# MLP weight preparation in three streams instead of one, with a bound on low parts per unit

## The chip, the cores and the metric

The kernel runs on one core of a Trainium2 chip. The metric is the device time of one execution in microseconds. The core has five engines with a queue of their own each: TensorE (PE in the profile, with its weight loads as PEld), VectorE (DVE), ScalarE (ACT), GpSimd (POOL) and SyncE (SP), which here only issues transfers. Each engine executes its queue in the order in which the program was written; engines wait for one another by semaphores.

## The reference

One layer of an encoder on 1024 tokens of width 1024. All arithmetic is float32.

```python
u = rms_norm(x, norm1_g); proj = u @ w_in            # 1024 x 5120
...                                                  # attention, short convolution, gates
x = x + merged @ w_o
h = rms_norm(x, norm2_g) @ w_mlp_in                  # 1024 x 4096
x = x + jnp.square(jax.nn.relu(h)) @ w_mlp_out       # 4096 x 1024
```

The change touches only the last two lines, the MLP.

## The kernel before, in words

**Arithmetic.** Each float32 operand is split into a high and a low float16 part, and a product is taken as three products of parts (high-high, high-low, low-high). Both MLP products also go through a scheme with seven products of half-size blocks instead of eight; sums of blocks are formed before it, on weights and activations, and sums of results after it. So weights have to be prepared before TensorE can use them, and that preparation runs beside the matmuls of the work before.

**First product.** `w_mlp_in` is cut into 16 chunks, numbered 0 to 15. A chunk is computed by `quad(q)`: seven units, each a group of 12 matmuls of 512 columns into one of eight PSUM banks (`seven`, `unit`, L207). Chunks 0 and 1 go in two halves of 256 columns each (chunk 0, chunk 1, chunk 0, chunk 1), because the activations come in pairs of tokens. The seven results are taken out of PSUM in the order of units 0 to 6: a copy by ScalarE (L1613), then by VectorE L1594 (unit 1), L1599 (unit 2), none for unit 3, L1615 (unit 4), L1602 to L1604 (unit 5, which read the banks of units 5, 3 and 2) and L1607 (unit 6). A bank is used again eight allocations later. Behind unit 6 `h_done` issues, on the next units, Relu (L1559) and Square (L1561) on ScalarE, four sums (L1281) on GpSimd, for chunks 0 and 1 on VectorE, and a store of 1.8 MB to memory by SP (L1572). The result tile of a chunk is one of two buffers.

**Preparation of a chunk.** `sums1(q)`: scale the rows of the two weight tiles (eight ScalarE operations, L959), square and add them up (two, L968), four block adds on GpSimd (L1077), then three units later the sum column on VectorE (L939, L940). `scale_of`: some units later a one-column matmul with ones (L198) adds over the partitions; it takes a PSUM bank of its own from the same rotation. A unit later VectorE turns the sum into a power of two (L201, L437 to L444). `prep1(q)` then waits by `gate(q)` until the weight buffer is free (three buffers, so until chunk q - 3 has been emitted) and `forms_split` writes the parts: four high parts on ScalarE and four low parts on VectorE, alternating (L1094, L1090). Behind the second low part SP gets the loads of the next weight tiles (`load_upto`, L229; five tile buffers).

**Second product.** `prep2(s)`, s = 0 to 3, makes 28 operand pairs, seven for each s: squares (L1666, L1669), block sums on GpSimd (L1675, L1676), a scale as above, and for each pair a high and low part of the activations (L1701, L1703) and two halves of the weights (L1706, L1710). The activations of the second pair come by a load of their own (L1682). Each pair is used by four units, which start behind chunk 15.

**What sets the order.** The program is written by Python generators: `fg` holds those that finish work on results, `bg` those that prepare weights. After emitting the 12 matmuls of a unit, `unit` emits the evacuation of the unit before and then lets `fg` advance by some steps and `bg` by some ticks (two steps and five ticks in the first product). A tick advances the first generator of `bg`. If that yields `WAIT` and the flag `side` is set, the tick goes to the next generator; otherwise it is used up. `apart(mark, n)` yields `WAIT` until n units have been emitted since mark. In the kernel before, `side` is off in the MLP, and `bg` holds one sequence: `sums1(2)`, then `prep1(2)` with `sums1(3)` at its end, and so on to 15. `first2()` and `prep2(0)` are appended behind chunk 13.

Of the kernel before, what the change touches and what calls it, by code (L numbers as in the profile page):

```python
# [10 lines left out]
F32 = mybir.dt.float32  # L11
F16 = mybir.dt.float16
# [58 lines left out]
def encoder_block(ctx: ExitStack, tc: tile.TileContext, x, weights, cols, gqk, rel, masks, out):  # L71
# [66 lines left out]
    WAIT = "w"  # L138
# [35 lines left out]
        forced[0] = False  # L174

    late, units, forced, side, splitting = [], [0], [False], [False], [False]
    work = [0]

    def apart(mark, n=3, of=units):
        while of[0] < mark + n and not forced[0]:  # L180
            yield WAIT
# [22 lines left out]
    def unit(mms, post=None, steps=0, ticks=0):  # L204

        for ps, l, r, a, b in mms:
            T.matmul(ps, l, r, start=a, stop=b)  # L207
        units[0] += 1
        work[0] += len(mms) * mms[0][0].shape[-1]
        settle()  # L210
        if post:
            late.append(post)
        for i in range(max(steps, ticks)):
            if i < steps:
                step()
            if i < ticks:
                tick()

    def settle():
# [864 lines left out]
    def parts(todo, s, then):  # L1084

        prev = None
        for n, it in enumerate(todo + [None]):
            if prev:
                o, w = prev
                V.scalar_tensor_tensor(o(1), w, sc[:, s], o(0), op0=OP.mult, op1=OP.subtract)  # L1090
                then(n - 1)
            if it:
                o, w = it
                A.activation(o(0), w, AF.Copy, scale=sc[:, s])  # L1094
            prev = it
            yield
# [245 lines left out]

    def gate(i):
        while pe_done[0] < i - 2:
            yield

    def need(i):
        while i not in ready:
# [23 lines left out]
    def prep1(q):  # L1372

        ch = c1[q]
        s, ch.inv = yield from scale_of(ch.sum, 9, 1)
        yield from gate(q)
        pool, tag = TAGS[q % 3]
        P = P1[q] = pool.tile([128, 7 if q else 8, 2, 512], F16, name="w16_1", tag=tag)
        yield from forms_split(ch, tsum[q], s, P)
        ready.add(q)  # L1380
        if 1 < q < 15:
            yield from sums1(q + 1)

    SQJ = U2[1][:, 0, :, :, 384:512].rearrange("p s k t -> p (s k) t").bitcast(BF16)
    scaled = []
# [143 lines left out]
    def last_pair():  # L1529
        sq(7, 1)()  # L1530
        normal(7, row3(7))
        yield from wait(3)
        form_sums()
        high(3, 0), high(3, 1)
        yield from wait(6)
        low(3, 0)
        yield from wait(3)
        bg.append(sums1(2))
        bg.extend(prep1(q) for q in range(2, 16))
        yield from wait(6)  # L1540
        low(3, 1)
        limit[0] = 10 ** 6
        load_upto(done[0] + 5)
# [10 lines left out]
    def h_done(q, c0=0, c1=512, wait1=0, wait2=0):  # L1554

        f = AS[q] if c1 < 512 else AS.pop(q)
        v = f[:, :, c0:c1]
        yield from wait(wait1)
        A.activation(v[:, 0:4], v[:, 0:4], AF.Relu)  # L1559
        yield  # L1560
        A.activation(v[:, 0:4], v[:, 0:4], AF.Square, scale=sc[:, c1w[q].inv],  # L1561
                     accum_out=sc[:, at(bsum[q // 4], 4 if c1 < 512 else q % 4)])
        yield
        yield from wait(wait2)
        if q > 1:
            yield from sums(v, G)
        else:
            for _ in sums(v, V):
                pass
        if c1 < 512:  # L1570
            return
        SP.dma_start(HS[q // 4][:, :, q % 4], f)  # L1572
        live.remove(q)
        if q % 4 == 3:
            m = tmp()
            V.tensor_reduce(sc[:, m], sc[:, bsum[q // 4]], axis=AX, op=OP.max)
            yield
            yield from pow2(m, 14, *R[q // 4])
            r_ready[q // 4] = True

    def quad(q, c0=0, c1=512):
        need(q)
        if c0 == 0:
            while q - 2 in live:
# [12 lines left out]

        def post5(ps):
            V.tensor_tensor(z[1], ps[5], z[5], op=OP.subtract)  # L1599

        def post7(ps):
            V.tensor_tensor(z[6], ps[7], z[5], op=OP.add)  # L1602
            V.tensor_tensor(z[2], ps[4], z[6], op=OP.add)  # L1603
            V.tensor_tensor(z[3], ps[5], z[6], op=OP.subtract)  # L1604

        def post3(ps):
            V.tensor_tensor(z[1], ps[3], z[1], op=OP.add)  # L1607
            if q == 0:
                fg.append(h_done(q, c0, c1, 3, 4 if c0 else 24))
            elif c1 == 512:  # L1610
                fg.append(h_done(q, 0, c1, *((2, 6) if q == 1 else ())))
        seven(P1[q], actU2, c0, c1, {
            1: lambda ps: A.activation(z[4], ps[1], AF.Copy),  # L1613
            6: post6, 5: None if c0 else post5,
            2: lambda ps: V.tensor_tensor(z[0], ps[2], z[4], op=OP.add),  # L1615
            7: post7, 3: post3}, 2 if c1 == 512 else 3, 5, (1, 2, 5, 4, 6, 7, 3) if c0 else (1, 6, 5, 4, 2, 7, 3))

    def whole(q):
        quad(q)
        pe_done[0] = q + 1  # L1620
# [7 lines left out]
    quad(1, 256, 512)  # L1628
    pe_done[0] = 2
    held[0] = 0  # L1630
    for q in range(2, 14):
        whole(q)


    OPS, X2 = {}, {}
# [12 lines left out]

    ORDER = ((0, "w11"), (4, "t2"), (1, "w21"), (5, "t3"), (2, "t1"), (3, "t4"), (6, "w22"))

    def prep2(s):
        raw, x2 = c2[s].raw, X2[s]
        w11, w12 = raw[0:2], raw[2:4]
        w21, w22 = [x2[:, i] for i in range(2)], [x2[:, i] for i in range(2, 4)]
# [13 lines left out]
        for i in range(2):  # L1668
            A.activation(j, x2[:, 2 * i:2 * i + 2].rearrange("p a c -> p (a c)"), AF.Square, scale=sc[:, iR],  # L1669
                         accum_out=sc[:, at(sm, 4 + i)])  # L1670
            yield
        sums = sum_of(sm)
        T2 = later["t2"]()
        for i in range(2):
            G.tensor_tensor(T2[:, i], w12[i], w22[i], op=OP.add)  # L1675
            G.tensor_tensor(T2[:, i], T2[:, i], w11[i], op=OP.add)  # L1676
        yield
        if s == 0:
            yield from gate(17)
            P = OPS[17] = TAGS[17 % 3][0].tile([128, 2, 2, 2048], F16, name="ops", tag=TAGS[17 % 3][1])  # L1680
            later["h", 1] = P[:, 0].rearrange("p w m -> p (w m)").bitcast(F32).rearrange("p (k t) -> p k t", k=4)
            SP.dma_start(later["h", 1], HS[0][:, ORDER[1][0]])  # L1682
        sw, inv = yield from scale_of(sums, 0)
        fw = keep()
        mul(iR, sw, fw)
        c2[s].inv = inv
# [1 line left out]
        for o, (f, name) in enumerate(ORDER):  # L1688
            n = 7 * s + o
            i = 16 + n  # L1690
            yield from gate(i)
            pool, tag = TAGS[i % 3]
            if n > 1:
                OPS[i] = pool.tile([128, 2, 2, 2048], F16, name="ops", tag=tag)
            P = OPS[i]
            while ("h", n) not in later:
                yield
            if 1 < n < 25:
                h_load(n + 3)
            hf = later.pop(("h", n)).rearrange("p k t -> p (k t)")  # L1700
            A.activation(P[:, 1, 0], hf, AF.Copy, scale=sc[:, Rs])  # L1701
            yield
            V.scalar_tensor_tensor(P[:, 1, 1], hf, sc[:, Rs], P[:, 1, 0], op0=OP.mult, op1=OP.subtract)  # L1703
            w = {"w11": w11, "t1": w11, "t3": w12, "w21": w21, "w22": w22}.get(name) or [T2[:, i] for i in range(2)]
            for i2 in range(2):
                A.activation(P[:, 0, 0, 1024 * i2:1024 * i2 + 1024], w[i2], AF.Copy, scale=sc[:, fw])  # L1706
            yield
            for i2 in range(2):
                sl = slice(1024 * i2, 1024 * i2 + 1024)
                V.scalar_tensor_tensor(P[:, 0, 1, sl], w[i2], sc[:, fw], P[:, 0, 0, sl], op0=OP.mult, op1=OP.subtract)  # L1710
                yield
# [26 lines left out]
        later["t2"] = lambda: h0[:, 1].rearrange("p (a k) t -> p a (k t)", a=2)  # L1738
        yield from wait(12)

    bg.append(first2())
    bg.append(prep2(0))
    whole(14)
    whole(15)


    later["hf"] = base.tile([128, 4, 4, 512], F32, name="hf", tag="U")
# [129 lines left out]
```

## Time and profile before

| | |
|---|---|
| time, median of 3 runs | 1233.58 us (1231.42 to 1234.42) |
| profiled execution, its own time | 1232.41 us |
| its span | 1230.6 us |
| granted TensorE clock over the span | 0.994 |
| chunk 2 of the first product starts | 672.87 us into the span |
| first unit of the second product starts | 931.27 us |

Rows of the order of time read: start in us from the span's beginning, duration in us, engine, line, operation, output tile and input tiles, number of operations merged; in brackets the idle time before it on its engine and what ended that. A group of 12 matmuls of 512 columns is shown with 2.75 us, and the next group starts 2.59 us after it, as the matmuls overlap.

### The profile page before, as it was taken

The page shows a single profiled execution, that of the slowest core. Times are in us where ns is not written, and L with a number is a line of the kernel's source. Part 1 is how long each engine was busy: PE and PEld are TensorE (multiplying, and loading weights), DVE is VectorE, ACT ScalarE, POOL GpSimd, SP SyncE. Part 2 cuts the span into 40 slices and gives each one's busy share as a digit, 9 for nine tenths or more (in the row PEclk, how much of TensorE's full clock was granted, in tenths as well). Part 3 has the DMA queues.
Part 4 walks back from the last instruction along what each step waited for, and adds up shares of the span by engine and source line. Part 5 has one row for each costly group of instructions (what it writes and reads, how often), then busy time and mean ns, then how long its engine had stood idle before and what let it go on. Part 6 is the DMA issues. An engine that isn't in the chain of part 4 may idle for free.

```text
span 1230.6 us, 16688 instructions
## 1 busy us (share of the span) xinstructions
PE 1197.8 (97%) x6102; PEld 575.8 (47%) x6102; DVE 943.2 (77%) x1747; ACT 765.9 (62%) x1185; POOL 432.5 (35%) x289
## 2 busy tenths in 40 slices
PE   4989999999999999999999999999999999999998
PEld 3534445555444444444468444444444444444444
DVE  6668778898658686887878555455447899999997
ACT  6777667778645455436768687687775763646430
POOL 2340003231411111101004455665658463464562
PEclk9999999999999999999999999999999999999999
DMA  6457455567551121125197454355374924435202
GB/s 259 105 201 173 105 117 120 127 138 143 112 141 60 45 69 44 61 80 227 32 166 186 149 188 160 131 179 178 131 265 162 366 104 162 171 115 220 104 35 103
DMA packets 170867, 173.34 MB, mean 141 GB/s; under 512 B 131488, under 2 KB 132000, under 8 KB 166688
## 3 DMA queue, kind: packets, MB, share of 16 engines
q1 hardware_dynamic: 170784, 172.27, 47.0%
q8 instruction: 48, 0.79, 0.3%
q14 instruction: 35, 0.29, 0.1%
HBM read 102.51 MB, written 37.75 MB: 114 GB/s over the span
## 4 chain that ended last, share of the span: by engine, by line
PE 40%; DVE 7%; ACT 2%; issue 2%; DMA 1%; DVEq 0%; ACTq 0%
PE ps_d L207 16%; PE ps_s L207 13%; PE ps_o L207 10%; DVE ops L1710 1%; DVE w L1090 1%; DVE form L1281 1%; DVE v L1329 1%; DMA u2T<-v 1%; DMA u2x<-v 1%; DVE ops L1703 0%; DVE x L1464 0%; ACT ops L1701 0%; ACT as L1559 0%; DVE x L1808 0%; DVE as L1603 0%
## 5 line engine op out<-in xcount | busy, mean ns | idle before, releaser
L207 PEld LDWEIGHTS <-ops 128*128 128x128 f16 x1356 | 132.9, 98 | 161.0 <-issue 4.8
L207 PEld LDWEIGHTS <-w 128*128 128x128 f16 x1368 | 133.1, 98 | 143.9 <-issue 5.0
L927 PE MATMUL ps_d<-uT,w_ws 128*128 128x512 f16 x576 | 135.7, 379 | 2.0 <-DVE cv L66 2.0
L207 PE MATMUL ps_s<-ops 128*128 128x512 f16 (+1 forms) x528 | 118.4, 374 | 0.0
L207 PE MATMUL ps_d<-ops 128*128 128x512 f16 x504 | 115.6, 379 | 0.0
L207 PE MATMUL ps_d<-u2T,w 128*128 128x512 f16 (+1 forms) x504 | 110.1, 371 | 0.0
L1701 ACT ACTIVATE ops<-hf,sc 128x2048 f16<-128x2048 f32 x26 | 52.0, 1999 | 93.2 <-PE ps_d L207 51.4
L1077 POOL TENSOR_TENSOR tsum<-raw 128x512 f32<-128x512 f32 x28 | 46.5, 1676 | 148.8 <-ACT raw L959 148.8
L207 PEld LDWEIGHTS <-uT 128*128 128x128 f16 x648 | 64.6, 100 | 70.3 <-issue 6.6
L1281 POOL TENSOR_TENSOR as<-as 128x512 f32<-128x512 f32 x56 | 76.7, 1370 | 41.4 <-ACT as L1561 38.1
L207 PEld LDWEIGHTS <-w_s 128*128 128x128 f16 x588 | 56.9, 98 | 69.3 <-issue 0.9
L927 PEld LDWEIGHTS <-w_ws 128*128 128x128 f16 x576 | 55.6, 98 | 60.7 <-issue 2.6
L1703 DVE SCALAR_TENSOR_TENSOR ops<-hf,sc,ops 128x2048 f16<-128x2048 f32 x26 | 73.7, 2835 | 7.4 <-ACT ops L1701 7.4
L207 PE MATMUL ps_s<-u2x,w 128*128 128x512 f16 (+1 forms) x348 | 78.6, 375 | 0.0
L207 PE MATMUL ps_o<-ops 128*128 128x512 f16 x324 | 76.0, 385 | 2.4 <-DVE as L1604 2.4
L959 ACT ACTIVATE raw<-raw,sc 128x256 f32<-128x256 f32 x164 | 67.6, 493 | 11.1 <-DMA raw<-in_weights 11.1
L1077 POOL TENSOR_TENSOR gsum<-raw 128x512 f32<-128x512 f32 x14 | 18.7, 1353 | 128.1 <-ACT raw L959 74.4
L1094 ACT ACTIVATE w<-raw,sc 128x512 f16<-128x512 f32 (+1 forms) x28 | 24.7, 927 | 51.8 <-DVE sc L443 51.8
L1594 DVE TENSOR_TENSOR as<-ps_s,as 128x512 f32<-128x512 f32 x13 | 9.0, 691 | 57.9 <-ACT as L1613 57.9
L66 ACT ACTIVATE sz<-sz,sc 128x384 f32<-128x384 f32 (+1 forms) x64 | 37.2, 581 | 23.7 <-DVE sc L66 23.4
L207 PE MATMUL ps_o<-u2T,w 128*128 128x512 f16 (+1 forms) x204 | 45.9, 376 | 2.4 <-DVE as L1604 2.4
L207 PE MATMUL ps_d<-w_ws,uT 128*128 128x512 f16 x192 | 43.1, 379 | 1.4 <-DVE w_ws L300 1.4
(356 smaller groups left out, 2595.7 us busy)
## 6 DMA issues: line engine op xcount, KB each, us to landing
raw<-in_weights SPq DMA_DIRECT2D x89, 512.0 KB, 5.4
hs<-as SPq DMA_DIRECT2D x16, 1792.0 KB, 8.7
hf<-hs SPq DMA_DIRECT2D x26, 1024.0 KB, 5.0
w2x<-in_weights SPq DMA_DIRECT2D x16, 512.0 KB, 8.1
raw<-in_weights SPq DMA_DIRECT2D x16, 384.0 KB, 3.6
xt<-in_x SPq DMA_DIRECT2D x8, 512.0 KB, 10.0
gs<-s SPq DMA_DIRECT2D x4, 1024.0 KB, 6.2
x<-in_x SPq DMA_DIRECT2D x8, 512.0 KB, 10.2
```

Source lines behind the costliest of these rows:

```text
L66: return f(out, *a, **kw)
L207: T.matmul(ps, l, r, start=a, stop=b)
L927: T.matmul(ps, l, r, start=a, stop=b)
L959: A.activation(v, v, AF.Copy, scale=sc[:, at(g, 4 * i + k)])
L1077: G.tensor_tensor(t[:, o], a, b, op=OP.add)
L1090: V.scalar_tensor_tensor(o(1), w, sc[:, s], o(0), op0=OP.mult, op1=OP.subtract)
L1094: A.activation(o(0), w, AF.Copy, scale=sc[:, s])
L1281: sub.tensor_tensor(z[o], z[a], z[b], op=op)
L1329: V.tensor_tensor(v[:, :, 1], fv[0][:, a:b], v[:, :, 0], op=OP.subtract)
L1701: A.activation(P[:, 1, 0], hf, AF.Copy, scale=sc[:, Rs])
L1703: V.scalar_tensor_tensor(P[:, 1, 1], hf, sc[:, Rs], P[:, 1, 0], op0=OP.mult, op1=OP.subtract)
L1710: V.scalar_tensor_tensor(P[:, 0, 1, sl], w[i2], sc[:, fw], P[:, 0, 0, sl], op0=OP.mult, op1=OP.subtract)
```

## The change

The one sequence in `bg` becomes three generators with `side` set: `all_sums` (the sums of chunks 2 to 15), `all_scales` (their sum matmuls and scales) and `all_preps` (the parts; at its end `side` is switched off, and `first2` and `prep2(0)` follow in the same generator). `all_sums` starts a chunk when the chunk three before it is ready, a given chunk has been emitted and both weight tiles have been asked for; from chunk 4 on it then lets two units pass. The sum matmul comes two units after the sum column instead of one. `gate` yields `WAIT`. `pace` bounds the low parts per unit: once `spent` reaches it, the unit's further ticks are left out; it is 2 in chunks 2 and 3, 1 in chunks 4 to 15 and off before and after. Chunk 1's four sums go to GpSimd at once instead of VectorE six steps later. In `prep2(0)` the sum column waits until seven units have passed since `first2` ended, the sum matmul comes one unit after it instead of three, and the buffer and load of the second operand pair's activations come two units ahead of that pair's first operation instead of ahead of the scale.

```diff
@@ unit
+        spent[0] = 0
         for i in range(max(steps, ticks)):
             if i < steps:
                 step()
-            if i < ticks:
+            if i < ticks and (not pace[0] or spent[0] < pace[0]):
                 tick()
@@ parts (and both L1703 and L1710 in prep2)
                 V.scalar_tensor_tensor(o(1), w, sc[:, s], o(0), op0=OP.mult, op1=OP.subtract)
+                spent[0] += 1
@@ gate
         while pe_done[0] < i - 2:
-            yield
+            yield WAIT
@@ prep1
-        s, ch.inv = yield from scale_of(ch.sum, 9, 1)
+        while q > 1 and q not in scale1:
+            yield WAIT
+        if q > 1:
+            s = scale1.pop(q)
+        else:
+            s, ch.inv = yield from scale_of(ch.sum, 9, 1)
...
-        if 1 < q < 15:
-            yield from sums1(q + 1)
+
+    summed, scale1 = set(), {}
+
+    def all_sums():
+        for q in range(2, 16):
+            while q > 4 and q - 3 not in ready:
+                yield WAIT
+            while pe_done[0] < {2: 0, 3: 1, 4: 2}.get(q, q - 4) or len(c1[q].raw) < 2:
+                yield WAIT
+            if q > 3:
+                yield from apart(work[0], 2 * 6144, work)
+            yield from sums1(q)
+            summed.add(q)
+
+    def all_scales():
+        for q in range(2, 16):
+            while q not in summed:
+                yield WAIT
+            scale1[q], c1[q].inv = yield from scale_of(c1[q].sum, 9, 2)
+
+    def all_preps():
+        for q in range(2, 16):
+            yield from prep1(q)
+        side[0] = False
+        yield from first2()
+        yield from prep2(0, work[0])
@@ last_pair
-        bg.append(sums1(2))
-        bg.extend(prep1(q) for q in range(2, 16))
+        side[0] = True
+        bg.extend([all_sums(), all_scales(), all_preps()])
@@ h_done
-        if q > 1:
+        if q > 0:
             yield from sums(v, G)
@@ quad
-                fg.append(h_done(q, 0, c1, *((2, 6) if q == 1 else ())))
+                fg.append(h_done(q, 0, c1, *((2, 0) if q == 1 else ())))
@@ prep2
-    def prep2(s):
+    def prep2(s, mark=0):
...
+        yield from apart(mark, 7 * 6144, work)
         sums = sum_of(sm)
...
-        if s == 0:
-            yield from gate(17)
-            P = OPS[17] = TAGS[17 % 3][0].tile([128, 2, 2, 2048], F16, name="ops", tag=TAGS[17 % 3][1])
-            later["h", 1] = P[:, 0].rearrange("p w m -> p (w m)").bitcast(F32).rearrange("p (k t) -> p k t", k=4)
-            SP.dma_start(later["h", 1], HS[0][:, ORDER[1][0]])
-        sw, inv = yield from scale_of(sums, 0)
+        sw, inv = yield from scale_of(sums, 0, 3 if s else 1)
...
-            if n > 1:
+            if n:
                 OPS[i] = pool.tile([128, 2, 2, 2048], F16, name="ops", tag=tag)
             P = OPS[i]
+            if n == 1:
+                later["h", 1] = P[:, 0].rearrange("p w m -> p (w m)").bitcast(F32).rearrange("p (k t) -> p k t", k=4)
+                SP.dma_start(later["h", 1], HS[0][:, ORDER[1][0]])
+                yield from apart(work[0], 2 * 6144, work)
@@ the loop over the chunks
-    for q in range(2, 14):
-        whole(q)
...
-    bg.append(first2())
-    bg.append(prep2(0))
-    whole(14)
-    whole(15)
+    for q in range(2, 16):
+        pace[0] = 2 if q < 4 else 1
+        whole(q)
+    pace[0] = 0
```

More of the change, by code (lines that the diff above doesn't have):

```diff
@@ L176, in encoder_block @@
     late, units, forced, side, splitting = [], [0], [False], [False], [False]
-    work = [0]
+    work, spent, pace = [0], [0], [0]
     def apart(mark, n=3, of=units):
@@ L1703, in prep2 @@
             V.scalar_tensor_tensor(P[:, 1, 1], hf, sc[:, Rs], P[:, 1, 0], op0=OP.mult, op1=OP.subtract)
+            spent[0] += 1
             w = {"w11": w11, "t1": w11, "t3": w12, "w21": w21, "w22": w22}.get(name) or [T2[:, i] for i in range(2)]
@@ L1710, in prep2 @@
                 V.scalar_tensor_tensor(P[:, 0, 1, sl], w[i2], sc[:, fw], P[:, 0, 0, sl], op0=OP.mult, op1=OP.subtract)
+                spent[0] += 1
                 yield
```

## The prediction

> **What bounds the kernel now.** I read the page's part 1 first, then TensorE's order of time through the MLP, looking for idle time and slow restarts, and then the engines that those waits name. A unit is written chunk.unit: 3.2 is unit 2 of chunk 3; "output n" is the n-th operand pair behind chunk 15.
>
> ```profile
> span 1230.6 us, 16688 instructions
> PE 1197.8 (97%) x6102; PEld 575.8 (47%) x6102; DVE 943.2 (77%) x1747; ACT 765.9 (62%) x1185; POOL 432.5 (35%) x289
> ```
>
> TensorE is the bound, so the change can give at most what TensorE waits in the stretch that it touches. Its order of time there:
>
> ```profile
> 672.87 2.75 PE L207 MATMUL ps_d<-u2T,w 128*128 128x512 f16 x12
> 691.03 2.75 PE L207 MATMUL ps_d<-u2T,w 128*128 128x512 f16 x12
> 693.62 2.75 PE L207 MATMUL ps_s<-u2x,w 128*128 128x512 f16 x12
> 698.78 4.44 PE L207 MATMUL ps_o<-u2T,w 128*128 128x512 f16 x12 [2.41 <-DVE as L1604]
> 703.05 2.75 PE L207 MATMUL ps_d<-u2T,w 128*128 128x512 f16 x12
> 931.27 2.75 PE L207 MATMUL ps_o<-ops 128*128 128x512 f16 x12
> 936.46 2.75 PE L207 MATMUL ps_s<-ops 128*128 128x512 f16 x12
> 941.60 4.44 PE L207 MATMUL ps_o<-ops 128*128 128x512 f16 x12 [2.39 <-DVE as L1604]
> 945.88 2.75 PE L207 MATMUL ps_d<-ops 128*128 128x512 f16 x12
> 993.35 0.18 PE L198 MATMUL ps_d<-ones 128*128 128x1 bf16 x1 [0.69 <-DVE ones L940]
> 318.00 1.67 PE L927 MATMUL ps_d<-uT,w_ws 128*128 128x512 f16 x7 [2.04 <-DVE cv L66]
> ```
>
> Units follow each other at 2.59 us (691.03, 693.62). 672.87 starts chunk 2, 691.03 chunk 3, 931.27 the first output. Unit 3.2 loses 703.05 - 693.62 - 2 x 2.59 = 4.25 us, the fourth unit of output 0 loses 945.88 - 936.46 - 5.18 = 4.24. Both times the matmul waits for the last reader (L1604) of its bank. About 2.5 us is the wait; 1.7 is a slow restart (12 matmuls in 4.44 instead of 2.75). After an idle time of 2.04 us (318.00) seven matmuls took 1.67, no slowdown. So 2.04 us costs only itself, 2.39 costs 1.7 more. The row at 993.35 is a small wait of the sum matmul, outside what the change reorders.
>
> Why L1604 came late, from VectorE's order of time:
>
> ```profile
> 689.43 2.96 DVE L1090 SCALAR_TENSOR_TENSOR w<-raw,sc,w 128x512 f16<-128x512 f32 x2
> 692.31 4.50 DVE L1090 SCALAR_TENSOR_TENSOR w<-tsum,sc,w 128x1024 f16<-128x1024 f32 x2
> 698.05 0.68 DVE L1604 TENSOR_TENSOR as<-ps_o,as 128x512 f32<-128x512 f32 x1
> 709.07 1.94 DVE L1090 SCALAR_TENSOR_TENSOR w<-raw,sc,w 128x512 f16<-128x512 f32 x2
> 710.92 2.47 DVE L1090 SCALAR_TENSOR_TENSOR w<-tsum,sc,w 128x1024 f16<-128x1024 f32 x2
> 923.57 4.50 DVE L1710 SCALAR_TENSOR_TENSOR ops<-raw,sc,ops 128x1024 f16<-128x1024 f32 x2
> 933.71 5.32 DVE L1710 SCALAR_TENSOR_TENSOR ops<-h,sc,ops 128x1024 f16<-128x1024 f32 x2 [1.28 <-ACT ops L1706]
> 941.47 0.68 DVE L1607 TENSOR_TENSOR as<-ps_s,as 128x512 f32<-128x512 f32 x1
> ```
>
> Four low parts of one chunk stand together ahead of the evacuation, 7.4 us while POOL works (689.43 to 696.81), 4.3 while it does not (709.07 to 713.39). The chunks from 709 on lose nothing. So the most to be gained is 4.25 + 4.24 = 8.5 us.
>
> **The change part by part.** The work stays the same, except that chunk 1's four sums move from VectorE to POOL. What moves is each queue's order. Counted through the yields, five ticks per unit, I get this order after the change: chunk 2's low parts in the third half-unit of chunk 0's second half (two half-units later); chunk 3's sums only when that half is done, its lows in 2.4 and 2.5 (before: ahead of chunk 2); chunk 4's sums in 2.2; chunk 5's sums in 3.0, its sum column in 3.3, its sum matmul in 3.5; chunk 4's lows in 3.3 and 3.4; chunk 6's sums in 3.6, its sum matmul in 4.4; chunk 5's lows one per unit, 4.1 to 4.4. From chunk 5 on a chunk's round takes six units of seven, so the lead grows until gate() stops it. ScalarE, VectorE and SP keep to their order, and here the lead is gone. Durations:
>
> ```profile
> 678.43 1.90 ACT L1559 ACTIVATE as<-as 128x2048 f32<-128x2048 f32 x1
> 680.36 2.00 ACT L1561 ACTIVATE as<-as,sc 128x2048 f32<-128x2048 f32 x1
> 684.41 1.76 ACT L1094 ACTIVATE w<-raw,sc 128x512 f16<-128x512 f32 x2 [1.95 <-DVE sc L443]
> 686.08 2.17 ACT L1094 ACTIVATE w<-tsum,sc 128x1024 f16<-128x1024 f32 x2
> 688.16 3.29 ACT L959 ACTIVATE raw<-raw,sc 128x256 f32<-128x256 f32 x8
> 693.48 0.18 ACT L968 ACTIVATION_READ_ACCUMULATOR tsum<-raw 128x1 f32 x1
> 703.30 0.58 ACT L1613 ACTIVATE as<-ps_d 128x512 f32<-128x512 f32 x1
> 686.66 2.86 DVE L1281 TENSOR_TENSOR as<-as 128x512 f32<-128x512 f32 x4
> 704.52 0.14 DVE L939 TENSOR_REDUCE sc<-sc 128x1 f32<-128x2 f32 x1
> 705.88 0.16 DVE L201 TENSOR_SCALAR sc<-ps_s 128x1 f32<-128x1 f32 x1 [0.43 <-PE ps_s L198]
> 706.71 0.14 DVE L444 TENSOR_SCALAR sc<-sc 128x1 int32<-128x1 int32 x1
> 703.48 5.32 POOL L1281 TENSOR_TENSOR as<-as 128x512 f32<-128x512 f32 x4 [5.54 <-ACT as L1561]
> 716.22 2.62 POOL L1077 TENSOR_TENSOR tsum<-tsum,raw 128x512 f32<-128x512 f32 x2 [0.44 <-ACT tsum L968]
> 689.60 0.53 SPq L1572 DMA_DIRECT2D hs<-as  x1
> 690.18 3.06 SPq L229 DMA_DIRECT2D raw<-in_weights  x3
> raw<-in_weights SPq DMA_DIRECT2D x3, 512.0 KB, 9.2
> ```
>
> So Relu and Square take 4.1, row scaling 3.3, with the squares 5.5 (688.16 to 693.66), four high parts 3.8, POOL's sums 5.3, half its adds 2.6, the small operations of a scale 1.0 (705.88 to 706.85), a sum column with its cast 0.35 (from 704.52), and a load that shares the engines with a store lands after 9.2 us.
>
> *Chunk 2.* The copy of 2.0 ends at 676.2 (its unit ends at 675.5). Relu and Square of chunk 1 end at 680.3, rows and squares of chunk 4 at 685.8, chunk 3's highs at 689.6. Its lows start at 686.5, after the first high; POOL has 10.6 us of work from 680.3 (chunk 1's sums, chunk 4's adds), so they take 7.4, with L1615 and the sum column 8.4: the last one ends at 694.9. Unit 3.1 needs it behind its first matmul, at 693.8: wait 1.0 (none if POOL does not slow them). The posts of 2.5 and 2.6 take four times 0.6: L1607 ends at 697.4 (694.3).
>
> *Chunk 3.* Chunk 5's loads are now issued with chunk 3's second low part, in 2.4, on SP behind the store of chunk 1, which waits for POOL's sums (691 to 694). They land 9.2 us after about 693.3: 702.5. "Two units" is 5.2 us. ScalarE in 3.0 has Relu (behind L1607, to 699.3), the first rows (load: 702.5 to 704.1), Square (706.3), the second rows (708.0), the squares (710.3), and only then 3.0's copy L1613 (710.8). VectorE waits for that copy with L1594; behind it stand the five small operations of chunk 4's scale, L1599 and chunk 5's sum column, 2.5 us: 713.3. The sum matmul stands on TensorE behind 3.5, which ends at 691.03 + 6 x 2.59 + 1.0 = 707.6. Wait 5.7 and a slow restart, 7.4. With every row at its fast end it is 711.6 against 706.6, 6.7 with the restart.
>
> *Chunk 4.* Of chunk 5's adds on POOL two wait for the squares (710.3, to 712.9); chunk 2's sums stand behind (718.2, or 721 while lows run), then its store, then on SP the loads for chunk 6: landed at 728. ScalarE meets them in 3.6, ahead of chunk 3's Relu: second rows and squares to 732, Relu and Square 736, a high part 0.7 and 4.0's copy 737.3. L1594 and the sum column: 738.3. TensorE, restarted at 713.3, ends 4.4 at 713.3 + 1.7 + 6 x 2.59 = 730.5. Wait 7.7, with the restart 9.4. Then the loads no longer stand behind a store of their own unit (pace 1), ScalarE has about 14 of 18 us to do per chunk, and I find no further wait; where rows fall on unit 0 again (chunk 9) the column is about 1 us early.
>
> *The end.* Output 0's lows come in 15.2 to 15.4, output 1's in the first output unit, so nothing holds up chunk 15's L1604: 4.24 gained. But output 1 is due at the fifth unit, 10.36 us on. In the trace before output 2 has that place:
>
> ```profile
> 946.12 1.99 ACT L1701 ACTIVATE ops<-hf,sc 128x2048 f16<-128x2048 f32 x1
> 948.14 2.93 DVE L1703 SCALAR_TENSOR_TENSOR ops<-hf,sc,ops 128x2048 f16<-128x2048 f32 x1 [1.36 <-ACT ops L1701]
> 950.99 4.51 DVE L1710 SCALAR_TENSOR_TENSOR ops<-w2x,sc,ops 128x1024 f16<-128x1024 f32 x2
> ```
>
> After L1607's end (942.15) the first weight half was done 11.1 us later, the second 13.3. With L1607 ending 0.9 us into output 0, the second matmul of output 1 waits for 12.0 - 10.6 = 1.4, later ones 0.9 more: 2.3; if POOL delays L1607 by 1 us the idle time reaches 2.4, and with a restart it is 5.0. I take 3.5.
>
> On the restart the Trainium skill (TensorE: Matmul & The Clock Gate, Part 1) states that the clock halves after at least one idle window of about 3.4 us. The rows at 698.78 and 941.60 differ: 2.4 us were enough. By the page the end would cost 3.3 at most and the two long waits the same.
>
> Other edits: the first sum matmul is no longer late, but a transpose holds the next unit there: nothing. POOL's 5.3 us for chunk 1 is counted; VectorE's 2.9 saved there lies in the same backlog.
>
> **Sum.** -4.25 + 1.0 + 7.4 + 9.4 - 4.24 + 3.5 = +12.8. The profiled execution took 1232.41, the median is 1.2 above it: 1245.2, I say 1245.
>
> **Rivals.** (1) *Faster*: VectorE keeps up because POOL slows nothing and the loads land early. It decides at one point: chunk 5's sum column written before 706.6. Then 8.5 is gained and 2.3 paid at output 1: 1226.2. For it: VectorE was busy only 77%. Against it: the 9.2 us of a load behind a store. (2) *One new wait, not two*: chunk 6's loads are in when ScalarE gets to them: -4.25 + 1.0 + 7.4 - 0.7 = +3.5, 1235.9. For it: the third step rests on the two before. (3) *The old waits stay in another form and cancel*: within 2 us, 1232 to 1235. (4) *The lag does not dissolve*, and each round costs a wait of about 10 us for one to three more chunks: 1255 to 1275. Against it: ScalarE's four spare us per chunk.
>
> **Numbers.** About 0.3% (3.7 us) is what a measurement tells from no change here. Chances: forecast 0.44, (1) 0.18, (2) 0.21, (3) 0.07, (4) 0.10. Slower: 0.44 + 0.10 + half of (2), 0.65; within: the other half and most of (3), 0.16; faster: 0.19. The range takes in the forecast's ends (1239 with the end at 2.3 and short waits, 1250), (2), (3) and half of (1) and (4): 1226 to 1258; the forecast alone has 1239 to 1250.
>
> **What would show it.** Right: no idle time behind L1604 in chunk 3 and output 0; idle time of TensorE in front of sum matmuls (L198, waiting for L940) in chunks 3 and 4; ScalarE's row scaling waiting for the loads there; a wait of the fifth output unit for L1710. Wrong: the loads of chunk 5 landing before ScalarE reaches them, the copy L1613 of chunk 3 before 703, or an order of emission that differs from my count.

## The result and the profile after

The changed kernel takes 1271.64 us (median of 4 runs, 1271.00 to 1272.57) against 1232.94 us (4 runs) of the kernel before on the same chip: ratio 1.0313, 95% interval 1.0296 to 1.0329. It is 38.7 us slower. The profiled execution took 1272.57 us, and its span is 40.2 us longer than before.

From the page of the changed kernel, span and part 1:

```profile
span 1270.8 us, 16705 instructions
...
PE 1205.1 (95%) x6102; PEld 576.9 (45%) x6102; DVE 952.8 (75%) x1743; ACT 765.2 (60%) x1185; POOL 447.4 (35%) x293
```

TensorE is still the bound and has the same 6102 matmuls, but its share has gone from 97% to 95%. Part of the extra time even counts as busy, since slow restarts do (1205.1 for 1197.8). Code lines lie further down in the changed kernel: Relu is L1590, Square L1592, ScalarE's copy L1644, the store L1603, the row scaling L960. In the runs with a later store, the store and what follows it lie two lines further, and in e8 Relu is L1561 and the copy L1615. TensorE's order of time in the changed kernel, at the four sum matmuls that came late and at the fifth unit of the second product:

```profile
706.21 2.75 PE L207 MATMUL ps_d<-u2x,w 128*128 128x512 f16 x12
715.90 0.16 PE L198 MATMUL ps_s<-ones 128*128 128x1 bf16 x1 [6.94 <-DVE ones L941]
715.93 4.80 PE L207 MATMUL ps_o<-u2x,w 128*128 128x512 f16 x12
720.57 1.67 PE L207 MATMUL ps_d<-u2T,w 128*128 128x512 f16 x7
743.18 0.16 PE L198 MATMUL ps_d<-ones 128*128 128x1 bf16 x1 [8.61 <-DVE ones L941]
743.21 4.81 PE L207 MATMUL ps_s<-u2x,w 128*128 128x512 f16 x12
747.86 2.75 PE L207 MATMUL ps_o<-u2x,w 128*128 128x512 f16 x12
842.30 0.16 PE L198 MATMUL ps_o<-ones 128*128 128x1 bf16 x1 [3.50 <-DVE ones L941]
846.60 1.67 PE L207 MATMUL ps_s<-u2T,w 128*128 128x512 f16 x7
870.71 0.16 PE L198 MATMUL ps_s<-ones 128*128 128x1 bf16 x1 [11.00 <-DVE ones L941]
870.73 4.21 PE L207 MATMUL ps_o<-u2x,w 128*128 128x512 f16 x12
975.86 2.75 PE L207 MATMUL ps_o<-ops 128*128 128x512 f16 x12
983.80 2.72 PE L207 MATMUL ps_d<-ops 128*128 128x512 f16 x6 [2.90 <-DVE ops L1740]
992.06 1.24 PE L207 MATMUL ps_d<-ops 128*128 128x512 f16 x5
```

Read losses from starts, at 2.59 us a unit: from 706.21 to 720.57 two units passed, so 720.57 - 711.39 = 9.2 us were lost. Where the row of the unit ahead isn't shown, the wait counts with 0.19 us for the overlap of groups and the sum matmul, and what the next unit took over 2.59 (behind 870.73 the next unit starts at 874.77). The balance, against the trace before:

| place | predicted | measured |
|---|---|---|
| ahead of chunk 2 (a transfer of activations went out 2 us later there) | 0 | +2.0 |
| old wait in unit 3.2 | -4.25 | -4.25 |
| units 3.1, 4.1, 4.2 (695.66: 0.2; the others 0.9) | +1.0 | +1.1 |
| sum matmul after 3.5 (715.90) | +7.4 | +9.2 |
| sum matmul after 4.4 (743.18): 8.61 + 0.19 + 2.06 | +9.4 | +10.9 |
| two sum matmuls in chunks 9 and 10 (842.30, 870.71): 5.4 and 12.6 | 0 | +18.0 |
| old waits in output 0 and behind it (993.35 before) | -4.24 | -5.1 |
| output 1 (975.86 to 992.06, three units in 16.20 us) | +3.5 | +8.4 |
| sum | +12.8 | +40.3 |

Behind the sum matmuls stands the sum column of VectorE (L941, line 940 before). ScalarE's order of time in the changed kernel:

```profile
698.77 1.91 ACT L1590 ACTIVATE as<-as 128x2048 f32<-128x2048 f32 x1 [7.43 <-DVE as L1638]
705.42 1.70 ACT L960 ACTIVATE raw<-raw,sc 128x256 f32<-128x256 f32 x4 [4.74 <-DMA raw<-in_weights]
712.82 0.58 ACT L1644 ACTIVATE as<-ps_o 128x512 f32<-128x512 f32 x1
835.51 1.71 ACT L960 ACTIVATE raw<-raw,sc 128x256 f32<-128x256 f32 x4 [2.15 <-DMA raw<-in_weights]
860.06 1.70 ACT L960 ACTIVATE raw<-raw,sc 128x256 f32<-128x256 f32 x4 [14.82 <-DMA raw<-in_weights]
```

Part 5 of its page has the whole group of the row scaling: busy time and mean ns of one, then the idle time ahead of it and what ended that:

```profile
L960 ACT ACTIVATE raw<-raw,sc 128x256 f32<-128x256 f32 x164 | 68.0, 495 | 43.4 <-DMA raw<-in_weights 43.4
```

VectorE's order of time there:

```profile
713.43 0.69 DVE L1625 TENSOR_TENSOR as<-ps_s,as 128x512 f32<-128x512 f32 x1 [14.70 <-ACT as L1644]
715.69 0.16 DVE L941 CAST ones<-sc 128x1 bf16<-128x1 f32 x1
```

And SyncE's:

```profile
695.16 0.52 SPq L1603 DMA_DIRECT2D hs<-as  x1
695.77 3.00 SPq L230 DMA_DIRECT2D raw<-in_weights  x3
850.52 0.52 SPq L1603 DMA_DIRECT2D hs<-as  x1
851.14 19.02 SPq L230 DMA_DIRECT2D raw<-in_weights  x3
```

GpSimd's last sums ahead of these two stores:

```profile
693.00 2.13 POOL L1283 TENSOR_TENSOR as<-as 128x512 f32<-128x512 f32 x1
842.48 8.02 POOL L1283 TENSOR_TENSOR as<-as 128x512 f32<-128x512 f32 x4
```

Read it backwards. TensorE waits for the sum column at 715.69. VectorE got there late because it stood 14.70 us in front of L1625, the first evacuation that needs ScalarE's copy L1644. ScalarE made the copy at 712.82, since it had stood 4.74 us in front of raw weights. Those weights were asked for at 695.77, right behind the store of 695.16, which went out as GpSimd's sums ended (693.00 + 2.13 = 695.13), and were scaled 9.7 us later. 155 us on it is the same: a load asked for at 851.14 behind the store of 850.52 (the sums ended at 842.48 + 8.02 = 850.50), 14.82 us of waiting on ScalarE, 11.00 on TensorE.

### The profile page after: what moved, and what is told of

Read it like the earlier page. It is cut to its first block, busy times and chain, and to the rows that moved or that the text cites. A ratio compares the mean times of both kernels' runs of the same rounds, so it can differ in the third digit from the quotient of the medians.

```text
span 1270.8 us, 16705 instructions
## 1 busy us (share of the span) xinstructions
PE 1205.1 (95%) x6102; PEld 576.9 (45%) x6102; DVE 952.8 (75%) x1743; ACT 765.2 (60%) x1185; POOL 447.4 (35%) x293
## 4 chain that ended last, share of the span: by engine, by line
PE 33%; DVE 6%; ACT 5%; DMA 4%; issue 3%; POOL 2%; SPq 0%; DVEq 0%; POOLq 0%; ACTq 0%
PE ps_s L207 12%; PE ps_d L207 12%; PE ps_o L207 8%; DMA raw<-in_weights 3%; DVE w L1091 2%; ACT raw L960 1%; ACT tsum L969 1%; POOL as L1283 1%; DMA ops<-hs 1%; DVE form L1283 1%; ACT as L1590 1%; DMA u2x<-v 1%; DVE ops L1740 1%; DVE v L1331 0%; ACT v L1326 0%
## 5 line engine op out<-in xcount | busy, mean ns | idle before, releaser
L1283 POOL TENSOR_TENSOR as<-as 128x512 f32<-128x512 f32 x60 | 104.2, 1737 | 73.5 <-ACT as L1592 70.1
L207 PE MATMUL ps_d<-ops 128*128 128x512 f16 x504 | 118.3, 384 | 5.4 <-DVE ops L1740 3.5
L960 ACT ACTIVATE raw<-raw,sc 128x256 f32<-128x256 f32 x164 | 68.0, 495 | 43.4 <-DMA raw<-in_weights 43.4
L1078 POOL TENSOR_TENSOR tsum<-raw 128x512 f32<-128x512 f32 x28 | 39.5, 1422 | 130.9 <-ACT raw L960 130.9
L1091 DVE SCALAR_TENSOR_TENSOR w<-raw,sc,w 128x512 f16<-128x512 f32 (+1 forms) x28 | 38.9, 1397 | 57.6 <-ACT w L1096 57.5
L207 PE MATMUL ps_d<-u2T,w 128*128 128x512 f16 (+1 forms) x372 | 80.0, 365 | 1.8 <-DVE as L1638 1.8
L1590 ACT ACTIVATE as<-as 128x2048 f32<-128x2048 f32 (+1 forms) x17 | 30.7, 1807 | 66.7 <-DVE as L1638 66.7
L207 PE MATMUL ps_s<-u2T,w 128*128 128x512 f16 (+1 forms) x276 | 58.1, 360 | 0.0
L207 PE MATMUL ps_s<-u2x,w 128*128 128x512 f16 (+1 forms) x216 | 50.7, 385 | 0.4 <-DVE w L1091 0.4
L1091 DVE SCALAR_TENSOR_TENSOR w<-tsum,sc,w 128x1024 f16<-128x1024 f32 x28 | 46.5, 1673 | 5.7 <-ACT w L1096 5.7
## 6 DMA issues: line engine op xcount, KB each, us to landing
xt<-in_x SPq DMA_DIRECT2D x8, 512.0 KB, 10.3
```

The source lines that it names most:

```text
L960: A.activation(v, v, AF.Copy, scale=sc[:, at(g, 4 * i + k)])
L1078: G.tensor_tensor(t[:, o], a, b, op=OP.add)
L1283: sub.tensor_tensor(z[o], z[a], z[b], op=op)
```

## The experiments

*Theory A*: the loads stand on SP behind a store that waits for POOL's sums; they land late; ScalarE, which works in order, waits for them in front of an evacuation copy. *Rivals*: B, the row sums begin too late against their chunk whatever the loads do; C, the bound of low parts per unit is to blame. D and E are stated where they come up.

**e1, the store two units later**, so that the loads go ahead of it:

```diff
+        if q:
+            yield from wait(4)
         SP.dma_start(HS[q // 4][:, :, q % 4], f)
```

> The changed kernel with one edit: from chunk 1 on, each store of the high words (L1603) is issued two units later, so that the weight loads of the same unit stand ahead of it in SP's queue. Theory A (the loads stand behind the store, the store behind POOL's sums; ScalarE then waits for the late loads with the row scaling L960, VectorE for ScalarE's copy L1644, and the sum column L941 comes late): ScalarE's 43.4 us of waiting for raw weights falls to under 15 us, the three late sum matmuls of 9.2, 10.9 and 12.6 + 5.4 us mostly go, and the time falls from 1271.6 to 1235 to 1250 us. Rival B (the lead is lost at the start of each row-sum stretch whatever the loads do): waits for raw weights may shrink, but the matmul waits stay above 25 us in all and the time at 1262 us or more.

Measured 1240.66 us (1239.88 to 1242.87), ratio 1.0071 (1.0045 to 1.0098). The row scaling on its page:

```profile
L960 ACT ACTIVATE raw<-raw,sc 128x256 f32<-128x256 f32 x164 | 67.9, 495 | 10.3 <-DMA raw<-in_weights 10.3
```

SyncE's order of time in e1:

```profile
691.14 0.33 SPq L230 DMA_DIRECT2D raw<-in_weights  x1
694.43 0.53 SPq L1605 DMA_DIRECT2D hs<-as  x1
```

TensorE's, at its late sum matmuls:

```profile
710.33 0.16 PE L198 MATMUL ps_s<-ones 128*128 128x1 bf16 x1 [2.10 <-DVE ones L941]
710.36 4.44 PE L207 MATMUL ps_o<-u2x,w 128*128 128x512 f16 x12
824.86 0.16 PE L198 MATMUL ps_o<-ones 128*128 128x1 bf16 x1 [2.44 <-DVE ones L941]
841.56 0.16 PE L198 MATMUL ps_s<-ones 128*128 128x1 bf16 x1 [0.98 <-DVE ones L941]
```

And ScalarE's at the activations of output 1, which e6 takes up:

```profile
943.39 2.00 ACT L1732 ACTIVATE ops<-ops,sc 128x2048 f16<-128x2048 f32 x1 [0.94 <-DMA ops<-hs]
```

The load now goes out 3.3 us ahead of the store instead of behind it. ScalarE's wait falls from 43.4 to 10.3 us, the wait of 8.61 is gone and those of 6.94, 3.50 and 11.00 are 2.10, 2.44 and 0.98. ScalarE's 10.3 us are no remainder: the kernel before has 11.1 us of it, and in the stretch of the MLP 0.7 us are left here. By the ratios (1.0313 and 1.0071) two lines give back some 30 of the 38.7 us. So A is the main cause. The wait of 2.10 us in chunk 3 stays although the weights are there: Relu starts at 698.04, the row scaling of the next weights and their squares follow, and the copy comes at 707.26. That much of B holds; e8 takes it up. C is the next run.

**e2, no bound on the low parts** (`pace[0] = 0` in the loop over the chunks):

> The changed kernel without the bound of one or two low parts for a unit, the three streams kept. Theory A: the sum matmuls of chunks 3, 4, 9 and 10 still wait 6 to 12 us each, time 1262 to 1278 us. Rival C (the bound itself makes the parts late): these waits go and the time is 1235 to 1248 us.

Measured 1261.59 us, ratio 1.0241 (1.0210 to 1.0271), just under A's window. ScalarE still waits 38.0 us for raw weights, and sum matmuls still wait 28.3 us for their columns, but elsewhere: 4.8 in chunk 3, 4.8 in chunk 4, 11.5 in chunk 6 (791.53). From the start of chunk 2 to the first output unit this kernel takes 292.0 us, the changed one 293.2. So the bound does not cause the waits; it decides in which chunk they fall. What fell away was not foreseen: the second product loses nothing here.

**e3, four units instead of two between load and row sums** (`apart(work[0], 4 * 6144, work)` in `all_sums`):

> The changed kernel with four units instead of two between the issue of the weight loads and the row sums that use them. Theory A: a load that lands up to 8 us late is still there in time, ScalarE's waiting for raw weights falls from 43.4 us to under 15 us, the sum matmuls' waits mostly go, and the time is 1235 to 1250 us (more if the longer lead makes a chunk's weights late). Rival B: the waits stay and the time is 1262 us or more.

Measured 1264.07 us, ratio 1.0261 (1.0229 to 1.0292): outside A's range, although ScalarE's wait fell to 13.2 us, chunks 9 and 10 lost nothing, and chunks 2 to 4 lost 9.4 us instead of 21.1. The output operands became late instead, with waits of 10.04, 3.78 and 10.28 us at outputs 0 and 1. The note in brackets ("more if the longer lead makes weights late") was the case that happened, at the operands of the second product.

**e4, the end as before** (no seven units ahead of the scale, the second pair's activations loaded early, sum matmul three units behind its column):

> The changed kernel with the preparation of the output weights as before (the activations of the second operand loaded ahead of the scale, into a buffer of their own, no distances between scale and halves), the rest changed. The 8.4 us that the trace of the changed kernel shows ahead of the fifth output unit go; the wait of 4.2 us at the fourth output unit of the kernel before may come back: 1263 to 1268 us. If the end's loss has its cause earlier (output weights late because the streams before run late), the time stays at 1270 us or more.

Measured 1270.73 us, ratio 1.0315 (1.0284 to 1.0346): a miss. The second product still loses 8.6 us, 7.1 of them at outputs 0 and 1, with a wait of 4.15 us for L1740 one unit further on. The activations of output 1 were scaled 1.9 us ahead of the first output unit here (964.58 against 966.45), so neither their load nor the changed order of the end makes this loss by itself. With the run without the bound this points to the bound: *theory E*.

**e5, the store on GpSimd's own queue**, at its old place:

```diff
-        SP.dma_start(HS[q // 4][:, :, q % 4], f)
+        G.dma_start(HS[q // 4][:, :, q % 4], f)
```

> The changed kernel with one edit: the stores of the high words (L1603) are issued on GpSimd's own queue, at the same place of the program, so that no weight load stands behind them on SP. Theory A (what delays the loads is their place behind a store that waits for POOL's sums): the late sum matmuls go as they did with the later store, ScalarE waits under 15 us for raw weights, time 1236 to 1248 us. Rival D (the later store helped because it moved its traffic, not its place in the queue): the waits stay, 1260 us or more.

Measured 1252.89 us, ratio 1.0168 (1.0147 to 1.0188). The row scaling on its page:

```profile
L960 ACT ACTIVATE raw<-raw,sc 128x256 f32<-128x256 f32 x164 | 68.1, 495 | 10.8 <-DMA raw<-in_weights 10.7
```

A store in GpSimd's order of time:

```profile
793.59 0.90 POOL L1603 DMA_DIRECT2D hs<-as  x1
```

The traffic is the same and at the same place of the program; only the queue differs, and the wait for raw weights falls to 10.8 us as with the later store. D falls: the place in the queue is what counts. The time is 5 us above the range. At 809.72 and 829.78 sum matmuls wait 2.78 and 2.64 us with a slow restart each, though the loads are there, and outputs 0 and 1 lose 8.2 us more than in the kernel before. So late loads were not the only thing that can make a column late; more on that below.

**e6, the later store, and no bound from chunk 13 on** (`1 if q < 13 else 0`):

> The kernel with the later store (1240.7 us), and from chunk 13 on no bound on the low parts of a unit. Theory E (at the end the bound holds back the streams, so the operands of the first output units come late; it is no matter of the shared buffer): the end's 8.4 us against an undisturbed run of output units go, 1230 to 1234 us. If the end's loss comes from the shared buffer and the late load of the activations, the time stays at 1238 us or more.

Measured 1235.79 us (1235.51 to 1237.72), ratio 1.0030 (1.0018 to 1.0041). TensorE's order of time, in chunk 3 and at outputs 0 and 1:

```profile
711.61 0.16 PE L198 MATMUL ps_s<-ones 128*128 128x1 bf16 x1 [2.10 <-DVE ones L941]
711.64 2.75 PE L207 MATMUL ps_o<-u2x,w 128*128 128x512 f16 x12
941.10 2.75 PE L207 MATMUL ps_o<-ops 128*128 128x512 f16 x12
956.64 2.75 PE L207 MATMUL ps_d<-ops 128*128 128x512 f16 x12
```

ScalarE's, at the activations of output 1:

```profile
933.69 1.99 ACT L1732 ACTIVATE ops<-ops,sc 128x2048 f16<-128x2048 f32 x1
```

From 941.10 to 956.64 six units pass in 15.54 us: the end loses nothing. ScalarE scales output 1's activations at 933.69, 7.4 us ahead of the first output unit. With the bound it did so at 943.39, 5.9 us behind that unit, which started at 937.49 in the run with the later store. The shared buffer and its load are the same in both, so theory E stands: the bound leaves out a unit's further ticks, and with them all that the streams would have done. The time is 1.8 us over the range: waits of 2.10 us in chunk 3, 2.44 in chunk 4, 1.7 and 1.0 in chunks 9 and 10 and 1.6 at 917.77 are left.

**e7, the later store, no bound at all:**

> The kernel with the later store and no bound on the low parts at all. If the 28 us of waits for sum columns and the end of the unbounded kernel (1261.6 us) have the same cause, loads behind the store: 1228 to 1238 us. If the bound is needed to keep the evacuations in time: 1242 us or more.

Measured 1238.80 us, ratio 1.0053 (1.0033 to 1.0074), 0.8 above the range and beside the kernel with the bound up to chunk 12 (1235.79). The 11.5 us of chunk 6 are 1.7; waits of 1.3 to 2.4 us in other chunks are left. With the loads ahead of the stores the bound seems worth some 3 us, but the two ratios' intervals overlap (1.0033 to 1.0074 and 1.0018 to 1.0041), so that is not shown.

**e8, the bound alone in the kernel before** (2 in chunk 2, 1 in chunk 15):

> The kernel before with the bound alone, in two places: at most two low parts for a unit in chunk 2 and one in chunk 15, where its two waits of 4.2 us stand (each with a restart of some 1.7 us behind it in the same number). If low parts in a bunch ahead of the evacuations are the cause of these waits: both go, 1224 to 1228 us. If the bound only moves them, or holds the output operands back as theory E says of the end: 1230 to 1240 us.

Measured 1276.82 us, ratio 1.0363 (1.0346 to 1.0381), a plain miss and the most useful one. TensorE's waits (in all, times, longest):

```profile
PE ps_d L198 <- DVE ones L941: 27.1, 8, 3.8
...
PE ps_d L198 <- DVE sc L127: 9.9, 3, 3.8
```

Its order of time at two of them:

```profile
754.13 0.16 PE L198 MATMUL ps_d<-ones 128*128 128x1 bf16 x1 [3.01 <-DVE ones L941]
754.16 4.44 PE L207 MATMUL ps_s<-u2x,w 128*128 128x512 f16 x12
777.14 0.16 PE L198 MATMUL ps_d<-ones 128*128 128x1 bf16 x1 [3.01 <-DVE ones L941]
777.17 2.75 PE L207 MATMUL ps_s<-u2x,w 128*128 128x512 f16 x12
```

ScalarE's order of time at a chunk's end, a line of the kernel before ahead of three of e8:

```profile
699.36 1.91 ACT L1559 ACTIVATE as<-as 128x2048 f32<-128x2048 f32 x1 [5.70 <-DVE as L1607]
719.61 1.91 ACT L1561 ACTIVATE as<-as 128x2048 f32<-128x2048 f32 x1 [5.24 <-DVE as L1609]
721.43 1.69 ACT L960 ACTIVATE raw<-raw,sc 128x256 f32<-128x256 f32 x4
728.82 0.58 ACT L1615 ACTIVATE as<-ps_d 128x512 f32<-128x512 f32 x1
```

Eleven sum matmuls, every 22 to 23 us from 709 to 935, wait 37.0 us in all. No load is late here (ScalarE waits 10.5 us for raw weights over the whole kernel, 11.1 in the kernel before). Leaving out ticks in chunk 2 has moved the row scaling to the first unit of the next chunks. There it stands between Relu and the copy, which comes 9.2 us after Relu (719.61 to 728.82). In the kernel before the scaling stood ahead of Relu, and the copy came 3.9 us after Relu (699.36, and 703.30 in the prediction's fence). The sum column is late and TensorE waits. A round of the one stream takes the seven units of a chunk: in the trace before, the sum matmul stands behind unit 3 of every chunk from 2 to 13 and waits nowhere; here it stands behind unit 4 of every chunk from 3 to 13 and waits in each. A bound of two low parts a unit in one chunk has put the stream into a bad phase for the rest of the product. I call this the second mechanism. It fits the small waits of the runs with the loads in time as well (in chunk 3 of e1 the copy also comes 9.2 us after Relu), though there it was not tried by itself. The old wait in 3.2 did go.

**e9, two small parts of the change alone, in the kernel before** (chunk 1's sums on GpSimd without the pause; the new order of the end):

> The kernel before, one stream and no bound, with two parts of the change alone: the maxima sums of chunk 1 on POOL without the pause of six units, and the preparation of the output weights with its seven units ahead of the scale, the second operand's activations loaded later. The two stand 240 us apart and are read by place. If each part removes the wait of 4.2 us at its own place: 1224 to 1227 us. If the first wait is taken away only by the bound or the streams: 1227 to 1230 us. If the second operand then comes late by its own load: 1232 us or more.

Measured 1236.73 us, ratio 1.0030 (1.0014 to 1.0046). By place: at the old wait of 3.2 TensorE gains 4.3 us and nothing comes back up to chunk 15; at the end it loses 7.4 us against before. TensorE's order of time there:

```profile
944.73 5.01 PE L207 MATMUL ps_o<-ops 128*128 128x512 f16 x12 [9.26 <-DVE as L1604]
```

ScalarE's:

```profile
934.61 2.00 ACT L1701 ACTIVATE ops<-ops,sc 128x2048 f16<-128x2048 f32 x1 [15.81 <-DMA ops<-hs]
```

With one stream and the late load of output 1's activations, ScalarE stands 15.81 us for them, and the low parts of that pair keep VectorE from the evacuation. Here the late load does cost. Whether the seven units ahead of the scale add to it, this run does not separate.

**e10 to e12, three shifts of the row sums**, each on the kernel of 1235.79 us: three units of lead; four up to chunk 11; Relu one unit later.

> The kernel with the later store and the end free of the bound (1235.8 us), with three units instead of two between load and row sums. Under theory A the loads already precede the store, so a longer lead gains only the row scaling's remaining 11.4 us of waiting, little of which reaches TensorE: 1232 to 1237 us. If the place of the row sums against the chunk's units decides about the last waits (3.3 us in chunks 9 and 10, 2.1 and 2.4 us in chunk 3): these move or go, 1228 to 1240 us.

> The same with four units up to chunk 11, two from chunk 12 on. The four units without the later store had no wait in chunks 9 and 10, and lost 26 us at the end, where the output operands came late. If that end was the longer lead's alone, and the rest adds up: 1229 to 1234 us. If the streams stay behind to the end: 1240 us or more.

> The kernel with the later store and the end free of the bound, with the first of a chunk's finishing steps (the relu of L1590) one unit later for every chunk from 2 on. In the trace ScalarE stands 7 us in front of that relu while the row scaling waits behind it; put later, the scaling runs in this gap. If this head of the queue is what makes the evacuation copy late: the waits at the sum matmuls shrink, 1229 to 1235 us. If the finishing steps then come late for store and buffer: 1238 us or more.

Measured 1250.97 (ratio 1.0148, 1.0124 to 1.0172), 1241.75 (1.0073, 1.0052 to 1.0095) and 1247.12 us (1.0117, 1.0092 to 1.0142). All slower. In each the waits moved: to 7.04 us at 740.96 and 5.33 at 927.36; to 4.13 and 3.14 at 715.74 and 719.07 and 2.17 in the second product; to 5.64 at 810.55 and 3.15 at the fourth unit of output 0. ScalarE waited 10.9 to 12.8 us for raw weights in all three, about as in the kernel before (11.1), so late loads explain little of it; that these are waits of phase is argued, not shown. It also shows that the 11.4 us which e10's expectation set out to gain were hardly there: 0.8 us of them lie in the MLP. I found no shift that is right for all chunks.

**e13 and e14, what is left of the change in the kernel before.** First the sums of chunk 1 alone, then with them a bound of one in chunk 15:

> The kernel before with one part of the change alone: the maxima sums of chunk 1 on POOL without the pause of six units. The sum of the prediction took the first 4.2 us off with the streams and the bound in place. If this part alone removes that wait and leaves nothing behind, as the run of it together with the changed end showed up to the output units: 1227 to 1229 us. If POOL's or the rows' later work slips by it: 1231 us or more.

> The kernel before with that part and, in chunk 15 alone, at most one low part for a unit. Where the bound stood in chunk 15 of the kernel before, the wait of 4.2 us at the fourth output unit was gone and one of 1.6 us stood later. If the two add up: 1224 to 1226.5 us. If the bound gained there only because that kernel was 46 us late by then, with its preparation ahead of TensorE: 1228 us or more.

Measured 1229.05 us, 0.05 above its first range (ratio 0.9973, 0.9961 to 0.9984) and 1224.79 us (0.9942, 0.9929 to 0.9956), against 1231.97 us. Both beat both kernels; the second by 7.2 us over the kernel before. Of the fourth output unit, in TensorE's order of time of the first of them:

```profile
938.86 2.75 PE L207 MATMUL ps_o<-ops 128*128 128x512 f16 x12 [2.40 <-DVE as L1604]
```

The wait in 3.2 is gone, the wait at the fourth output unit stands, and goes with the bound in chunk 15: no wait over 0.15 us is left between chunk 4 and the end in the trace of e14.

## Why the prediction was wrong

The direction, the mechanism and the two late sum matmuls of the start were right: loads on SP behind a store that waits for POOL (e1 and e5 take them from there, and of 6.94 and 8.61 us some 2.1 and nothing are left), ScalarE waiting with the row scaling in front of the copy, VectorE behind the copy, TensorE in front of L198. The terms 7.4 and 9.4 measured 9.2 and 10.9; the waits were 6.94 and 8.61 us where 5.7 and 7.7 were worked out, the restarts 2.05 where I took 1.7. What I worked out as one wait in chunk 3 had two parts: 4.74 us of it ScalarE stood for the load, and 2.1 us stay without that.

- **The step that failed** is the sentence behind *Chunk 4*: "Then the loads no longer stand behind a store of their own unit (pace 1), ... and I find no further wait; where rows fall on unit 0 again (chunk 9) the column is about 1 us early". The trace shows loads behind a store again (851.14), the sum column late by 3.50 us in chunk 9 and 11.00 in chunk 10, and 18.0 us lost. I had followed the order of emission unit by unit for two chunks and then argued with a mean (14 of 18 us of ScalarE's work). But a round of the row sums takes six units and a chunk seven, as I had written myself. In the trace the sum matmuls stand behind units 3.5, 4.4, 5.3, 6.2, 7.1, 8.0, 8.6, 9.5 and 10.4: after six chunks the places of chunks 3 and 4 come back, and load and store, and rows and copy, meet again. The margin of 1 us that I found in chunk 9 was no larger than my errors on the first two waits (1.2 and 0.9 us).
- **The end**, 3.5, measured 8.4. I priced output 1 by the row of output 2, whose activations lie in a buffer of their own. Output 1's share one with its weight halves, so the chain is longer, and with the bound it began 6.2 us behind the first output unit (5.9 in e1). e4 and e6 show that the bound, not the buffer, makes most of this. The bound was counted as spacing of low parts only. That it leaves out every further tick of the unit, and so delays all three streams, I did not count.
- **The two gains of 4.2 us** came as forecast, but not from the streams, so that these two terms held in part by luck. The first comes from the sums of chunk 1 alone (e9, e13). The second goes with a bound in chunk 15 (e14) or with an end that is prepared early (e2, e6).
- **Rival 4**, given 0.10, is where the time fell. Its reason, that the lag does not dissolve, is half right: it dissolved after chunk 4 and came back in chunks 9 and 10. e8 shows the pure form, one wait per round to the end.
- **Ahead of chunk 2** 2.0 us were lost, where a transfer of activations went out 2 us later. From the start of chunk 0 to that of chunk 2 the trace before takes 37.6 us, that of the changed kernel 39.6, the others 36.7 to 39.4. e2 and e7 have the changed kernel's order up to there and took 37.9 and 36.7, so it is variation between executions.

About 27.5 us lie between the predicted and the measured sum: 18.0 for chunks 9 and 10, 4.9 for output 1, 3.3 for the sizes of the first two waits, 2.0 ahead of chunk 2, and 0.1 for the small waits of chunks 3 and 4, less 0.9 for the wait at 993.35.

Open is how the two mechanisms share chunks 9 and 10. In chunk 9 of the changed kernel the copy comes 11.5 us after Relu, 2.15 of them the wait for the load (835.51) and the rest the sequence of e8. With the loads in time 1.0 to 2.4 us of waits are left in the two, which need not be the same in a kernel whose streams run 20 us later. That the streams could be made to gain by another pairing of lead and bound is not excluded either; the kernels tried with them stayed at or above 1235.8 us.

## What to carry to other kernels

SyncE's transfers went out in the order of the program here: before prefetches are moved, look for the store that they will stand behind and what that store waits for. Putting the prefetches ahead of the store gave back some 30 us. When two loops with different periods share in-order engines, follow the order of emission over a whole beat of the periods, not over the first two rounds, and count a limit on one kind of work with everything that it holds back. And take a change apart before it is given up: of this one, two lines and a bound in one chunk gain 7.2 us.

## What the runs showed of the hardware

The restart of TensorE after a wait is not a threshold, as the prediction had it between 2.04 and 2.39 us. The same wait of 2.10 us at the same matmul was followed by twelve matmuls in 4.44 us in one run (710.36, the later store) and in 2.75 in another (711.64, the end free). In the kernel before with the bound, waits of 3.01 us were followed by 4.44 (754.16) and by 2.75 (777.17), and the one of 3.80 us at 709.13 by 2.75. The granted clock says the same: 0.61 over the unit at 754.16, 1.00 over the one at 777.17. The wait of 2.40 us in the last fence cost nothing more, where 2.39 cost 1.7 before. In the stretch of the MLP, over all the traces, the shortest wait with a slow restart was 1.94 us (three units of lead, at 717.16), and from 3.84 us on every wait had one. In between each wait should be priced with and without a restart (1.4 to 2.1 us for the four of the changed kernel). The Trainium skill (TensorE: Matmul & The Clock Gate, Part 1) names at least one idle window of about 3.4 us, in windows that run free of the kernel. A slow restart after 2.10 us does not agree with that; 3.80 us without one can, as it may lie across two windows.

Issuing a store of 1.8 MB from GpSimd took 0.90 us of that engine (793.59), against 0.52 on SyncE.
